# Both mixers' matmuls on pairs of float16 parts instead of pairs of float32r parts, and the first output projection's weights split during the heads

## The chip, the cores and the metric

The kernel runs on one NeuronCore of a Trainium2 chip. Its engines work side by side: TensorE (PE in the profile, with PEld for its weight loads), VectorE (DVE), ScalarE (ACT), GpSimd (POOL) and SyncE (SP, which issues most DMAs). The metric is the device time of one execution in microseconds. Lower is better.

## What is computed

Two layers of a diffusion backbone on 1024 latent tokens and 128 context tokens of width 1024. Layer 0 mixes tokens with a bidirectional gated linear recurrence, layer 1 with a chunked spatial gating; a mixture of experts (MoE) follows each. Cut to what matters here:

```python
LRU_WIDTH = 1280   # 10 heads of 128
def _rglru_mixer(h, h0, w_in, conv_w, conv_b, w_a, b_a, w_x, b_x, lam, w_out):
    proj = h @ w_in
    gate = gelu(proj[..., :LRU_WIDTH])
    xb = _centred_depthwise_conv(proj[..., LRU_WIDTH:], conv_w, conv_b)
    for d in range(2):
        r = sigmoid(einsum('bthi,hij->bthj', xh, w_a[d]) + b_a[d])
        i = sigmoid(einsum('bthi,hij->bthj', xh, w_x[d]) + b_x[d])
        log_a = -8.0 * r * softplus(-lam[d])
        u = sqrt(-expm1(2.0 * log_a)) * (i * xb)
        h_d, fin = _linear_scan(exp(log_a), u, h0[:, d], reverse=(d == 1))
    y = ((hs[0] + hs[1]) * gate) @ w_out

def _sgu_mixer(h, w_in, norm_g, w_s, b_s, w_out):
    proj = gelu(h @ w_in)                       # 1024 -> 4096
    u, v = proj[..., :2048], _rmsnorm(proj[..., 2048:], norm_g)
    sv = einsum('gpq,bnqgc->bnpgc', w_s, v) + b_s   # within chunks of 128 tokens
    return (u * sv) @ w_out                     # 2048 -> 1024
# each layer: x = x + g1 * mixer(norm(x));  x = x + g2 * moe(norm(x))
```

## The kernel before

Every product in float32 precision is made of three matmuls on two parts of each operand: hi*hi, hi*lo and lo*hi. A helper, split (and its copies in split_w, split_g and split_wo), makes the parts: ScalarE casts the raw tile to the part hi, VectorE or GpSimd subtracts hi from the raw tile to give lo. In the MoE the parts are float16 (whi, wlo, Sh, Sl, Hh, Hl; L1591 and L1597 split the weights, L1706 multiplies). In both mixers the parts are of the type F32R, four bytes each.

Mixer 0 puts channels on partitions and all 1152 tokens on columns, in three groups of 386 (with a few padding columns). After a prologue that turns and normalises x and makes the modulation, 24 modulated tiles hn are split (L116, L117), and the projections begin: product, L844 to L846, three matmuls for each of 8 blocks of the contraction and each of the 3 column groups, so 72 for one head's one half of w_in. A loop over the heads follows. In the turn of head h it projects head h+1's recurrent half (kind 1), convolves it (conv: ScalarE copies the PSUM result to xp at L869, VectorE makes xc at L871 to L873), makes head h's gate products (ri, L882 to L884, 4 x 9 matmuls) and sigmoids (L941, L943), projects head h-1's gelu half (kind 0), then ScalarE's tanh, exp and square root (L950 to L961), VectorE's decay and drive (L966 to L974), two scans (L893), their sum (L982), and the product with the gelu of head h-1 (L986, L991, L992), which GpSimd stores to DRAM as hg_d. Parts of the later modulation (mod_step) are put between. Which engine does what is fixed by the order of the code: each engine works its own instructions off in that order. The weights of w_in come in blocks of 512 KB in the order of the list "order"; load_w issues a load into one of two buffers wraw, split_w splits the oldest block and issues the next load; split_w is called twice in a head, split_g once, for the gate weights.

Behind the last head's gates stand its two projections (kind 0 of heads 8 and 9), 144 matmuls. During these and the rest of head 9, w_out's ten row blocks are loaded (wor, four buffers, L1051) and split (split_wo: ScalarE L1055, and VectorE or GpSimd L1056), each at a hand-chosen place. The output projection (ymm, L1126 to L1128) takes the tokens in 9 chunks of 128: 10 heads x 2 column halves x 3 matmuls of 512 columns. Its left operand is hg, loaded from DRAM, split, and for head 9 kept on the chip as hg9. A router and the MoE follow.

Mixer 1 puts tokens on partitions in its products uv (L1297 to L1299): 9 chunks of 128 tokens, 8 column blocks of 512, 8 contraction blocks, three matmuls each; weights sgwh and sgwl are split as they come (sgr). The v half is normalised and multiplied with the spatial weights (sv, L1406 to L1408, 256 columns), then gating with u (L1411), and the result is turned and stored to mt_d. The output projection (L1466 to L1468) makes the first 512 output columns of all chunks, then the second: for each chunk it loads m in four pieces from mt_d, splits them (L116, L117) and runs 48 matmuls of 512 columns.

## Time and profile before

| | |
|---|---|
| runs shown | 2682.14, 2679.63, 2677.31 us; median 2679.63 |
| profiled execution | 2680.47 us, of which the span from the first to the last instruction is 2678.7 |
| busy in the span | PE 2511.0 us (94%), DVE 1925.0 (72%), ACT 1631.0 (61%), POOL 310.3 (12%) |
| matmuls | 26054 |
| DMA traffic | 647 MB, 242 GB/s |
| mean granted clock of TensorE | 0.967 of the full one |

The stages by the order of time, from the profiled execution: prologue 0 to 57 us, head loop with its lead-in 57 to 421, first output projection to 571, router to 627, MoE of layer 0 to 1260, mixer 1 from 1275 to 1966, router, MoE of layer 1 from 2020 to the end.

The profile is read so: a busy share says how much of the time an engine worked, not whether the others waited for it. Matmuls are pipelined, so the listed duration of one is longer than the distance to the next; the distance between starts is the price. An idle time carries behind the arrow what ended it. Where a chain row names an engine, the end of the execution hung on it there.

### The profile page before, as it was taken

The numbers are of one execution on the slowest core, as the hardware profiler recorded it, in microseconds if no ns is written. First come the engines' busy times: TensorE is split into PE (matmuls) and PEld (weight loads), VectorE is DVE, ScalarE is ACT, GpSimd is POOL, SyncE is SP. The second block draws the span as 40 slices with busy tenths as digits, with TensorE's granted clock in tenths as the row PEclk, the third lists the DMA queues.
The fourth block names the chain that finished last, engine by engine and source line by source line (L and its number), as shares of the span: only waits on it lengthen the run. The fifth ranks groups of instructions, "written<-read, shape, count | busy, mean of one in ns | idle before, by whom it ended". The sixth has DMA issues, their size and how long they took to land.

```text
span 2678.7 us, 60563 instructions
## 1 busy us (share of the span) xinstructions
PE 2511.0 (94%) x26054; PEld 2280.8 (85%) x26054; DVE 1925.0 (72%) x2766; ACT 1631.0 (61%) x2338; POOL 310.3 (12%) x330
## 2 busy tenths in 40 slices
PE   6999998968999999997999999999969999999996
PEld 5888987858999999997777788878858999999996
DVE  6887786368999999996622233344578999989997
ACT  4766784337787877775523333333347777777774
POOL 1011003020000000001200100000120000000003
PEclk8999999978999999998999999999978999999998
DMA  8455215446999999995544433355557999999994
GB/s 305 150 183 168 69 42 198 143 186 234 360 346 359 352 350 335 352 362 165 170 157 154 160 127 110 113 186 184 175 201 283 353 359 346 356 350 338 354 350 181
DMA packets 317755, 647.19 MB, mean 242 GB/s; under 512 B 15362, under 2 KB 52790, under 8 KB 317486
## 3 DMA queue, kind: packets, MB, share of 16 engines
q1 hardware_dynamic: 291792, 564.30, 59.1%
q0 software_dynamic: 21136, 74.67, 8.7%
q10 hardware_dynamic: 4558, 4.35, 0.5%
q8 instruction: 204, 3.34, 0.5%
q14 instruction: 65, 0.53, 0.1%
HBM read 576.59 MB, written 66.68 MB: 240 GB/s over the span
## 4 chain that ended last, share of the span: by engine, by line
PE 60%; DVE 26%; ACT 7%; issue 4%; DMA 2%; POOL 1%; SPq 0%; DVEq 0%; POOLq 0%; ACTq 0%
PE mm L1706 19%; DVE wlo L1597 14%; PE uv L1297 5%; PE uv L1299 5%; PE uv L1298 5%; PE y L1466 2%; PE y L1468 2%; PE y L1467 2%; PE pj L844 2%; DVE Hl L1730 2%; PE pj L845 2%; PE pj L846 2%; DVE t L1722 2%; ACT Hh L1727 2%; PE y L1126 1%
## 5 line engine op out<-in xcount | busy, mean ns | idle before, releaser
L1706 PEld LDWEIGHTS <-whi 128*128 128x128 f16 x12288 | 990.0, 98 | 28.8 <-issue 23.9
L1597 DVE SCALAR_TENSOR_TENSOR wlo<-raw,whi 128x1024 f16<-128x1024 f32 x759 | 894.6, 1220 | 20.6 <-ACT whi L1591 20.5
L1706 PE MATMUL mm<-Sh,whi 128*128 128x144 f16 x4096 | 774.9, 227 | 3.7 <-ACT tmp L1652 1.7
L1706 PE MATMUL mm<-Sl,whi 128*128 128x144 f16 x4096 | 774.7, 226 | 1.0 <-DVE Sl L1664 0.9
L1706 PE MATMUL mm<-Sh,wlo 128*128 128x144 f16 x4096 | 774.8, 227 | 0.0
L1591 ACT ACTIVATE whi<-raw 128x1024 f16<-128x1024 f32 x759 | 755.2, 1060 | 0.0
L1706 PEld LDWEIGHTS <-wlo 128*128 128x128 f16 x6144 | 602.9, 98 | 14.3 <-issue 14.2
L1706 PE MATMUL mm<-Hh,whi 128*128 128x144 f16 x2048 | 389.9, 227 | 17.4 <-DVE Hh L1729 14.9
L1706 PE MATMUL mm<-Hl,whi 128*128 128x144 f16 x2048 | 388.7, 227 | 8.6 <-DVE Hl L1730 8.6
L1706 PE MATMUL mm<-Hh,wlo 128*128 128x144 f16 x2048 | 388.7, 227 | 0.0
L1297 PE MATMUL uv<-sgwh,h_hi 128*128 128x512 f32 x576 | 232.2, 403 | 0.0
L1299 PE MATMUL uv<-sgwh,h_lo 128*128 128x512 f32 x576 | 226.7, 393 | 0.0
L1298 PE MATMUL uv<-sgwl,h_hi 128*128 128x512 f32 x576 | 225.8, 392 | 0.0
L1303 ACT ACTIVATE uvo<-uv 128x512 f32<-128x512 f32 x72 | 43.0, 597 | 217.2 <-PE uv L1299 217.2
L1750 POOL DMA_INDIRECT x_d<-o,idx x31 | 57.9, 1869 | 959.7 <-ACT o L1749 928.6
L844 PE MATMUL pj<-hn_hi,wh 128*128 128x386 f32 x480 | 164.6, 343 | 1.9 <-ACT hn_hi L116 1.9
L846 PE MATMUL pj<-hn_hi,wl 128*128 128x386 f32 x480 | 164.1, 342 | 0.0
L845 PE MATMUL pj<-hn_lo,wh 128*128 128x386 f32 x480 | 163.9, 341 | 0.0
L1411 DVE SCALAR_TENSOR_TENSOR uvo<-sv,bs,uvo 128x256 f32<-128x256 f32 x72 | 31.5, 479 | 156.1 <-PE sv L1408 156.1
L1297 PEld LDWEIGHTS uv<-sgwh,h_hi 128*128 128x128 f32 x576 | 109.2, 189 | 31.4 <-ACT uvo L1303 10.1
L1299 PEld LDWEIGHTS uv<-sgwh,h_lo 128*128 128x128 f32 x576 | 108.8, 189 | 24.4 <-DVE h_lo L1290 0.4
L1316 DVE TENSOR_TENSOR uvo<-uvo,gain 128x512 f32<-128x512 f32 x36 | 24.9, 691 | 145.4 <-ACT uv L1315 145.4
(398 smaller groups left out, 4253.8 us busy)
## 6 DMA issues: line engine op xcount, KB each, us to landing
raw<-in_moe_w_gate_dram SPq DMA_DIRECT2D x64, 2048.0 KB
raw<-in_moe_w_up_dram SPq DMA_DIRECT2D x64, 2048.0 KB
raw<-in_moe_w_down_dram SPq DMA_DIRECT2D x62, 2048.0 KB
wm<-in_w_mod_dram SPq DMA_DIRECT2D x96, 512.0 KB
m<-mt_d SPq DMA_DIRECT2D x72, 256.0 KB
sgr<-in_sg_w_in_dram SPq DMA_DIRECT2D x32, 512.0 KB
win<-in_lru_w_in_dram SPq DMA_DIRECT2D x20, 512.0 KB
v_d<-uvo POOLq DMA_DIRECT2D x36, 256.0 KB, 2.5
```

What stands on the lines that cost most here:

```text
L844: PE.matmul(ps[:, i, 0:WP], wh[:, k], hi[k][:, cs], start=(k == 0), stop=False)
L845: PE.matmul(ps[:, i, 0:WP], wh[:, k], lo[k][:, cs], start=False, stop=False)
L846: PE.matmul(ps[:, i, 0:WP], wl[:, k], hi[k][:, cs], start=False, stop=(k == KD - 1))
L1297: PE.matmul(ps, hi[:, k, cs], th[:, k % 4], start=(k == 0), stop=False)
L1298: PE.matmul(ps, hi[:, k, cs], tl[:, k % 4], start=False, stop=False)
L1299: PE.matmul(ps, lo[:, k, cs], th[:, k % 4], start=False, stop=(k == KD - 1))
L1466: PE.matmul(ps, mh, th[:, j], start=(q == 0 and j == 0), stop=False)
L1467: PE.matmul(ps, mh, tl[:, j], start=False, stop=False)
L1591: A.activation(hi, block(n, b), AF.Copy, scale=UP)
L1597: V.scalar_tensor_tensor(lo, block(n, b), UP, ws[n, b][0], op0=OP.mult, op1=OP.subtract)
L1706: PE.matmul(ps[:, b, 0:144], w[:, k], x[:, k], start=(k == 0 and i == 0), stop=(k == KD - 1 and i == 2))
L1750: G.indirect_dma_start(out=x_d[0:NS, :], out_offset=bass.IndirectOffsetOnAxis(ap=idxs[:, e:e + 1], axis=0), in_=o, in_offset=None, compute ...
```

## The change

All matmul operands in the two mixers become pairs of float16 tiles. A new helper, split_up, scales while it splits: hi = float16(raw * by) on ScalarE, lo = raw * by - hi on VectorE as one instruction with two operations. Weights are scaled by UP (2 to the 8th), hg and m by DOWN (2 to the -4th); 1/UP comes back in the activations that read PSUM (conv, gates, both gelus), 1/(UP*DOWN) in the multiplications with the gate row of the residual and in the prompt chunk's copies (take). Where GpSimd does the subtraction, ScalarE scales the raw tile in place first and then casts it. In mixer 1, bs is scaled instead of copied, mt copied with a scale, the square for the norm gets a float32 tile of its own (junk1), and the weights of a block lie in one tile.

The output projection's weights become blocks of kind 2 of the list of loads: three wraw buffers, and in each head one more call of split_w behind the sum of the scans; one more after the loop. load_wo and split_wo are gone, with their places at the end. The pool of w_out's parts (l0o) is opened in front of the heads' pool. The first two weight blocks and the first gate block are split in one place, ahead of the modulated tiles.

```diff
+    def split_up(raw, hi, lo, by=UP, eng=V):
+        if eng is G:
+            A.activation(raw, raw, AF.Copy, scale=by)
+            A.copy(hi, raw)
+            G.tensor_tensor(lo, raw, hi, op=OP.subtract)
+            return
+        A.activation(hi, raw, AF.Copy, scale=by)
+        V.scalar_tensor_tensor(lo, raw, by, hi, op0=OP.mult, op1=OP.subtract)
...
-            V.tensor_mul(yps, yps, self.g1)
+            V.scalar_tensor_tensor(yps, yps, 1.0 / (UP * DOWN), self.g1, op0=OP.mult, op1=OP.mult)
...
-                    A.copy(t[:, cs[n]], yps[n])
+                    A.activation(t[:, cs[n]], yps[n], AF.Copy, scale=1.0 / (UP * DOWN))
...
-        order = [(1, 0), (1, 1)] + [b for h in range(1, NH - 1) for b in ((1, h + 1), (0, h - 1))]
-        order += [(0, NH - 2), (0, NH - 1)]
+        WRAW = 3
+        order = [(1, 0), (1, 1), (1, 2), (0, 0), (2, 0)]
+        order += [b for h in range(1, NH - 2) for b in ((1, h + 2), (0, h), (2, h))]
+        order += [(0, NH - 2), (0, NH - 1), (2, NH - 2), (2, NH - 1)]
+        whl = {}
...
+                if kind == 2:
+                    SP.dma_start(raw[b].rearrange("p k n -> p (k n)"), lru_w_out[0, rows(h)])
+                else:
+                    SP.dma_start(raw[b], win[:, :, kind * LW + P * h:kind * LW + P * (h + 1)])
-        def split_w(copy=A.copy, eng=V):
+        def split_w(eng=V):
             if to_split:
                 kind, h = b = to_split.pop(0)
-                wh = wp.tile([P, KD, P], F32R, tag="whi", name=f"wh{kind}_{h}", bufs=2)
-                wl = wp.tile([P, KD, P], F32R, tag="wlo", name=f"wl{kind}_{h}", bufs=2)
-                copy(wh, raw[b])
-                eng.tensor_tensor(wl, raw.pop(b), wh, op=OP.subtract)
-                ready[b] = wh, wl
+                if kind == 2:
+                    whl[h] = [op_.tile([P, D], F16, name=f"wo{s}{h}") for s in "hl"]
+                    split_up(raw.pop(b).rearrange("p k n -> p (k n)"), *whl[h])
+                else:
+                    wh = wp.tile([P, KD, P], F16, tag="whi", name=f"wh{kind}_{h}", bufs=2)
+                    wl = wp.tile([P, KD, P], F16, tag="wlo", name=f"wl{kind}_{h}", bufs=2)
+                    split_up(raw.pop(b), wh, wl, eng=eng)
+                    ready[b] = wh, wl
...
-        split_w(eng=G)
+        for _ in range(2):
+            split_w(G)
+        gg = split_g(0, G)
...
-        hi, lo = zip(*([hp.tile([P, W], F32R, name=f"hn_{s}{k}") for s in ("hi", "lo")] for k in range(KD)))
+        hi, lo = zip(*([hp.tile([P, W], F16, name=f"hn_{s}{k}") for s in ("hi", "lo")] for k in range(KD)))
...
-            if u == 3:
-                split_w(G.tensor_copy, G)
-        gg = split_g(0, G)
...
-            A.activation(flat(xp[:, 2:W + 2]), ps[:, :, 0:WP], AF.Identity)
+            A.activation(flat(xp[:, 2:W + 2]), ps[:, :, 0:WP], AF.Identity, scale=1.0 / UP)
...
             c.scan(1)
             c.add()
+            split_w()
             if h > 0:
                 G.dma_start(hg_d[h - 1], gated(h - 1, gt))
...
+        split_w()
         norm_cols(0, 2)
...
-        for i in range(4):
-            load_wo(i)
...
-        split_wo(0, G)
         gt = gelu(NH - 2, gps[0])
...
         c.scan(1)
-        split_wo(1, G)
         c.add()
-        split_wo(2, V)
-        split_wo(3, V)
-        split_wo(4, G)
         gt = gelu(NH - 1, gps[1])
-        split_wo(5, V)
         t = gated(NH - 1, gt)
...
-        split_wo(6, G)
-        split_wo(7, V)
-        split(t, *hg9)
+        split_up(t, *hg9, DOWN)
...
-        split_wo(8, G)
-        split_wo(9, V)
...
-        hi = hp.tile([P, KD, NT], F32R, name="h1_hi")
-        lo = hp.tile([P, KD, NT], F32R, name="h1_lo")
+        hi = hp.tile([P, KD, NT], F16, name="h1_hi")
+        lo = hp.tile([P, KD, NT], F16, name="h1_lo")
...
-            t = raw.pop((i, r))
-            A.copy(th, t)
-            eng.tensor_tensor(tl, t, th, op=OP.subtract)
+            split_up(raw.pop((i, r)), th, tl, eng=eng)
...
-            A.activation(o, ps, AF.Gelu_apprx_tanh)
+            A.activation(o, ps, AF.Gelu_apprx_tanh, scale=1.0 / UP)
...
-            A.copy(mt, ps.rearrange("p a b -> p (a b)"))
+            A.activation(mt, ps.rearrange("p a b -> p (a b)"), AF.Copy, scale=DOWN / UP)
```

VectorE at the end of one of the late turns of the head loop, before: wl is the low part of a block of w_in, hv the two scans, hs first their sum (L982) and then, of the head before, the product with the gelu; xc begins the next convolution.

```order
L647 TENSOR_TENSOR wl_7_3040<-win_7_2777,wh_7_3039 128x1024
L893 SCALAR_TENSOR_TENSOR hv_1_3045<-tau_1_2998,par,ti_1_2910 128x1024
L893 SCALAR_TENSOR_TENSOR hv_1_3045<-tau_1_2998,ti_1_2910 128x128
L982 TENSOR_TENSOR hs_3049<-hv_0_3033,hv_1_3045 128x1152
L991 TENSOR_TENSOR hs_2783<-hs_2783,gt_3031 128x1024
L992 TENSOR_TENSOR hs_2783<-hs_2783,gt_3031 128x128
L871 TENSOR_SCALAR xc_3131<-xp_3127,par 128x1158
```

The same place now, with the lines of the changed kernel (wol is the low part of a block of w_out):

```order
L127 SCALAR_TENSOR_TENSOR wl_7_3090<-win_7_2821,wh_7_3089 128x1024
L913 SCALAR_TENSOR_TENSOR hv_1_3095<-tau_1_3048,par,ti_1_2960 128x1024
L913 SCALAR_TENSOR_TENSOR hv_1_3095<-tau_1_3048,ti_1_2960 128x128
L1002 TENSOR_TENSOR hs_3099<-hv_0_3083,hv_1_3095 128x1152
L127 SCALAR_TENSOR_TENSOR wol_3102<-win_7_2833,woh_3101 128x1024
L1011 TENSOR_TENSOR hs_2827<-hs_2827,gt_3081 128x1024
L1012 TENSOR_TENSOR hs_2827<-hs_2827,gt_3081 128x128
L891 TENSOR_SCALAR xc_3187<-xp_3183,par 128x1158
```

One subtraction now stands between the sum and the gelu product; on ScalarE the cast woh stands behind the last cast wh, ahead of the next xp.

ScalarE at the end of the heads, before: tau is head 9's last step there, woh are casts of blocks of w_out, gt the gelus of heads 8 and 9, hgh the high parts of what the output projection multiplies, hg9h those of head 9.

```order
L970 ACTIVATE tau_1_3561<-tau_1_3561 128x1158
L1055 CAST woh_3557<-wor_3531 128x1024
L986 ACT_TABLE_LOAD
L986 ACTIVATE gt_3581<-pj_8_3368 128x1158
L116 CAST hgh_3589<-hgl_3529 128x1024
L116 CAST hgh_3589<-hs_3306 128x128
L1055 CAST woh_3555<-wor_3533 128x1024
L1055 CAST woh_3539<-wor_3535 128x1024
L1055 CAST woh_3541<-wor_3537 128x1024
L1055 CAST woh_3543<-wor_3579 128x1024
L986 ACTIVATE gt_3620<-pj_9_3441 128x1158
L1055 CAST woh_3545<-wor_3604 128x1024
```

The same place now:

```order
L990 ACTIVATE tau_1_3596<-tau_1_3596 128x1158
L1006 ACT_TABLE_LOAD
L1006 ACTIVATE gt_3612<-pj_8_3434 128x1158
L126 ACTIVATE hgh_3620<-hgl_3592 128x1024
L126 ACTIVATE hgh_3620<-hs_3364 128x128
L1006 ACTIVATE gt_3635<-pj_9_3507 128x1158
L126 ACTIVATE hg_xh<-hs_3633 128x1152
```

The casts of w_out are gone from the end; the gelu of head 9 follows directly on the last small part of hgh.

## Rows read from the trace of the kernel before

**Rows 1.** Page: the chain that ended last, share of the span by engine.

```profile
PE 60%; DVE 26%; ACT 7%; issue 4%; DMA 2%; POOL 1%; SPq 0%; DVEq 0%; POOLq 0%; ACTq 0%
```

**Rows 2.** Windows: us of the span, busy us (instructions) per engine, PEclk, DMA share, GB/s.

```profile
421.00:446.00 25.00, 17.05 (x59) 12.26 (x58) 19.79 (x13) 11.90 (x12) 15.07 (x7) 0.86 0.72 240
...
627.00:1262.00 635.00, 618.29 (x9601) 610.62 (x9599) 571.03 (x768) 490.73 (x670) 50.04 (x32) 0.99 0.93 331
```

**Rows 3.** Lines by shape: line, engine, operation, tiles, count, busy us, mean ns, idle before.

```profile
L1706 PEld LDWEIGHTS <-whi 128*128 128x128 f16 x12288 | 990.0, 98 | 28.8 <-issue 23.9 <-DVE Sh L1661 3.2 <-DVE pt L1737 1.2
...
L1297 PE MATMUL uv<-sgwh,h_hi 128*128 128x512 f32 x576 | 232.2, 403 | 0.0
...
L844 PE MATMUL pj<-hn_hi,wh 128*128 128x386 f32 x480 | 164.6, 343 | 1.9 <-ACT hn_hi L116 1.9
...
L1466 PE MATMUL y<-sgwh,m_3hl 128*128 128x512 f32 x72 | 29.3, 407 | 0.1
```

**Rows 4.** TensorE in order of time: start us, duration us, line, tiles; pairs for pitches.

```profile
395.48 0.34 PE L846 MATMUL pj<-hn_hi,wl 128*128 128x386 f32 x1
...
420.38 0.33 PE L846 MATMUL pj<-hn_hi,wl 128*128 128x386 f32 x1
...
446.40 0.39 PE L1127 MATMUL y<-wol,hgh 128*128 128x512 f32 x1
...
452.81 0.40 PE L1128 MATMUL y<-woh,hg9l 128*128 128x512 f32 x1
...
1249.83 0.23 PE L1706 MATMUL mm<-Hh,whi 128*128 128x144 f16 x1
...
1252.45 0.38 PE L1744 MATMUL oTT<-ident,oT 128*128 128x128 f32 x2
...
1514.11 0.39 PE L1299 MATMUL uv<-sgwh,h_lo 128*128 128x512 f32 x1
...
1521.59 0.40 PE L1299 MATMUL uv<-sgwh,h_lo 128*128 128x512 f32 x1
```

**Rows 5.** Waits from 86 to 396 us (total, times, longest), then ScalarE in order.

```profile
ACT xp L869 <- PE pj L846: 67.5, 8, 9.9
...
DVE tau L966 <- ACT sq L961: 39.3, 9, 4.9
...
328.73 1.14 ACT L869 ACTIVATE xp<-pj 128x1158 f32<-128x1158 f32 x1 [6.69 <-PE pj L846]
...
361.55 1.14 ACT L869 ACTIVATE xp<-pj 128x1158 f32<-128x1158 f32 x1 [6.68 <-PE pj L846]
```

**Rows 6.** Lines by shape: splits of weight blocks in the MoE and in mixer 0.

```profile
L1597 DVE SCALAR_TENSOR_TENSOR wlo<-raw,whi 128x1024 f16<-128x1024 f32 x759 | 894.6, 1220 | 20.6 <-ACT whi L1591 20.5
...
L1591 ACT ACTIVATE whi<-raw 128x1024 f16<-128x1024 f32 x759 | 755.2, 1060 | 0.0
...
L647 DVE TENSOR_TENSOR wl<-win,wh 128x1024 fp32r<-128x1024 f32 x18 | 22.0, 1221 | 10.5 <-ACT wh L646 10.5
```

**Rows 7.** Order of time at the end of the heads: ScalarE, TensorE, then VectorE.

```profile
420.73 3.88 ACT L1055 CAST woh<-wor 128x1024 fp32r<-128x1024 f32 x4
...
425.69 0.80 PE L1126 MATMUL y<-woh,hgh 128*128 128x512 f32 x1 [4.28 <-ACT gt L986]
...
410.92 4.32 DVE L893 TENSOR_TENSOR_SCAN hv<-tau,par,ti 128x1024 f32<-128x1024 f32 x1
...
421.06 2.35 DVE L893 TENSOR_TENSOR_SCAN hv<-tau,par,ti 128x1024 f32<-128x1024 f32 x1
```

**Rows 8.** VectorE in order of time, mixer 1's output projection, first half of columns.

```profile
1769.19 0.69 DVE L262 TENSOR_TENSOR y<-y,g 128x512 f32<-128x512 f32 x1
...
1816.30 0.69 DVE L262 TENSOR_TENSOR y<-y,g 128x512 f32<-128x512 f32 x1
```

**Rows 9.** VectorE and ScalarE in order of time, ahead of the first projection.

```profile
47.98 2.32 DVE L776 TENSOR_SCALAR sp<-par 128x20 f32<-128x20 f32 x1
...
56.22 0.71 ACT L808 ACTIVATE hn<-hT,modc,ns 128x386 f32<-128x386 f32 x1 [8.38 <-DVE ns L188]
```

More of the change, by code (lines that the diff above doesn't have):

```diff
@@ L275, in residual @@
             cs = slice(512 * n, 512 * (n + 1))
-            V.tensor_mul(t[:, cs], yps, self.g1 if self.apart else self.g1[:, cs])
+            V.scalar_tensor_tensor(t[:, cs], yps, 1.0 / (UP * DOWN), self.g1 if self.apart else self.g1[:, cs],
+                                   op0=OP.mult, op1=OP.mult)
             V.tensor_add(xt[:, cs], xt[:, cs], t[:, cs])
@@ L686, in lru_mixer @@
             mod0.load(k)
-        for _ in range(2):
+        for _ in range(WRAW):
             load_w()
@@ L829, in lru_mixer @@
         e1.close()
+        op_ = pool_of(es, "l0o")
         tp = pool_of(es, "l0t")
@@ L874, in conv @@
                                        op0=OP.mult, op1=OP.add)
-            return xc, tmp("xh", f"xh{h}", dt=F32R), tmp("xl", f"xl{h}", dt=F32R)
+            return xc, *(tp.tile([P, W], F16, tag=tag, name=f"{tag}{h}", bufs=1) for tag in ("xh", "xl"))
         def ri(h, d, j, xh, xl, gh, gl):
@@ L940, in gates @@
                     tr = self.tr[d] = tmp("tr", f"tr{h}_{d}", 2)
-                    A.activation(flat(tr), ri(h, d, 0, xh, xl, *gg)[:, :, 0:WP], AF.Sigmoid, bias=par_of(50, d, h))
+                    A.activation(flat(tr), ri(h, d, 0, xh, xl, *gg)[:, :, 0:WP], AF.Sigmoid, bias=par_of(50, d, h), scale=1.0 / UP)
                     ti = self.ti[d] = tmp("ti", f"ti{h}_{d}", 2)
-                    A.activation(flat(ti), ri(h, d, 1, xh, xl, *gg)[:, :, 0:WP], AF.Sigmoid, bias=par_of(70, d, h))
+                    A.activation(flat(ti), ri(h, d, 1, xh, xl, *gg)[:, :, 0:WP], AF.Sigmoid, bias=par_of(70, d, h), scale=1.0 / UP)
                     V.tensor_mul(ti, ti, xc)
@@ L985, in gelu @@
             gt = tmp("gt", f"gt{h}")
-            A.activation(flat(gt), gps[:, :, 0:WP], AF.Gelu_apprx_tanh)
+            A.activation(flat(gt), gps[:, :, 0:WP], AF.Gelu_apprx_tanh, scale=1.0 / UP)
             return gt
@@ L1042, in lru_mixer @@
         carry = carry_of(0)
-        eo, ew = ExitStack(), ExitStack()
+        ew = ExitStack()
         pb = pool_of(ew, "l0b", side="right")
-        op_ = pool_of(eo, "l0o", 1, side="right")
-        whl, wor, hgs = {}, {}, {}
-        def load_wo(h):
-            if h < NH:
-                wor[h] = op_.tile([P, D], F32, tag="wor", name=f"wor{h}", bufs=4)
-                SP.dma_start(wor[h], lru_w_out[0, rows(h)])
-        def split_wo(h, eng):
-            wh, wl = whl[h]
-            A.copy(wh, wor[h])
-            eng.tensor_tensor(wl, wor[h], wh, op=OP.subtract)
-            load_wo(h + 4)
+        hgs = {}
         def load_hg(ch, h0=0, h1=9):
@@ L1065, in split_hg @@
         def split_hg(ch):
-            hh = tmp("ae", f"hgh{ch}", 2, F32R)[:, 0:9 * P].rearrange("p (h t) -> p h t", t=P)
-            hl = tmp("hs", f"hgo{ch}", 2, F32R)[:, 0:9 * P].rearrange("p (h t) -> p h t", t=P)
-            split(hgs[ch], hh, hl)
+            hh = tmp("ae", f"hgh{ch}", 2, F16)[:, 0:9 * P].rearrange("p (h t) -> p h t", t=P)
+            hl = tmp("hs", f"hgo{ch}", 2, F16)[:, 0:9 * P].rearrange("p (h t) -> p h t", t=P)
+            split_up(hgs[ch], hh, hl, DOWN)
             return hh, hl
@@ L1072, in lru_mixer @@
         SP.dma_start(hgs[0][:, 0:8], hg_d[0:8, :, rows(0)].rearrange("h p t -> p h t"))
-        for i in range(4):
-            load_wo(i)
-        for h in (*range(2, NH), 1, 0):
-            whl[h] = [op_.tile([P, D], F32R, name=f"wo{s}{h}") for s in "hl"]
         c.tanh()
@@ L1259, in norm @@
             for i, ch in enumerate(chs):
-                A.activation(hi[:, :, rows(ch)], xs[ch].rearrange("p (k t) -> p k t", k=KD), AF.Square,
-                             accum_out=ss[:, i:i + 1])
+                A.activation(junk, xs[ch], AF.Square, accum_out=ss[:, i:i + 1])
             r = sm.tile([P, 2], F32, tag="rstd2", name=f"rstd1_{chs[0]}")
```

46 lines of the change are left out of this document (22 added, 24 removed).

## The prediction, made before the changed kernel was run

> **What bounds the kernel now.** I read three views first. The chain that ended last gives TensorE 60% of the span and VectorE 26% [rows 1]; most of the VectorE part is the splitting of the experts' weights in the two MoE stages, which the change doesn't touch: there the windows show TensorE and VectorE busy side by side and the DMA engines at 0.93 [rows 2]. In the two mixers the chain runs through the matmul lines. The lines kept apart by shape then say how many matmuls of which width there are, all on four-byte operands [rows 3], and the order of time says how far apart two of them start [rows 4]. A listed mean (343 ns for 386 columns) is a latency, since matmuls overlap; what counts is the pitch from start to start.
>
> Pitches at the full clock [rows 4]: 386 columns, (420.38 - 395.48)/141 steps = 176.6 ns; 512 columns in the gating mixer, (1521.59 - 1514.11)/33 = 226.7 ns; in the first output projection, (452.81 - 446.40)/28 = 228.9 ns; 144 float16 columns in the MoE, (1252.45 - 1249.83)/42 = 62.4 ns. At TensorE's upper level, 2.4 GHz, one column per cycle would take 160.8, 213.3, 213.3 and 60.0 ns. So the four-byte matmuls lose 13 to 16 ns each, the float16 one 2.4 ns.
>
> The head loop of mixer 0 is bound by TensorE as well: ScalarE waits for the projection in front of a head's first step (L869), 67.5 us in 8 waits of up to 9.9 us, 6.69 us before one of the shortest heads, and VectorE waits 39.3 us in 9 waits in front of L966 [rows 5]. The shortest heads follow each other at 361.55 - 328.73 = 32.8 us [rows 5].
>
> **Matmuls on float16.** The change keeps the number of matmuls and columns and changes the operand width. No row of before shows a float16 matmul of 386 or 512 columns. The nearest is the 144-column one. Either what it loses over its columns is fixed (2.4 ns), so that 386, 256 and 512 columns take 163.2, 109.1 and 215.7 ns; or it grows with the width (62.4/60.0), which gives 167, 111 and 222 ns; at best nothing is lost, 160.8, 106.7 and 213.3. I take the fixed one: it is the middle of the three, and the three four-byte pitches lose about the same (13.4, 15.6, 15.8 ns) whatever their width. Saved per matmul: 13.4 ns at 386 columns, 11.0 in the gating mixer, 13.2 in the first output projection. For the 256-column ones (216) I show no pitch; they lie between 0 and 11 ns, I take 7.
>
> The Trainium skill, "TensorE: Matmul & The Clock Gate", section Back-to-back issue gap, gives N/2.4 + 2.5 ns from one matmul to the next, a fixed loss; by it the estimate would be the sum below, about 66 us, where a loss that grows would leave about 43. The 62.4 ns of the 144 columns [rows 4] agrees with it (62.5), but one width can't tell the two apart.
>
> Now by stage, for the profiled execution of 2680.5 us (span 2678.7 and 1.8 us around it; 0.8 above the median of 2679.6):
>
> Head loop. The projections are 3 x 480 matmuls of 386 columns (L844 to L846, of which one line is shown) [rows 3], 144 per head. Seven full head periods save 144 x 13.4 = 1.9 us, and about 0.3 more of the 36 gate matmuls (4 x 9 in the code), the rest of whose 0.5 ScalarE's gates hide: 7 x 2.2 = 15.4. The first 144, before the loop, reach the chain with 1.3; head 0, half as many, with 1.2. Together 17.9 us. Against this stands the added split of one weight block per head: a cast on ScalarE, 1.06 us, and a subtraction on VectorE, 1.22 us by the nearest forms, those of the MoE's splits [rows 6], and one load on SP's queue. ScalarE has 6.7 us of waiting in front of its next step there. VectorE meets the split behind the sum of a head's two scans, ahead of the gating product and the next convolution; they come 1.2 us later, and the wait in front of L966 (39.3/9 = 4.4 us) takes that up. In the shortest heads VectorE then needs 32.8 - 4.4 + 1.2 = 29.6, TensorE 32.8 - 2.2 = 30.6. So I cost the splits at nothing, but the cover left is about 1 us. Splits that were there cost the same: VectorE's old form takes 1221 ns, the new 1220 [rows 6].
>
> End of the heads. Before, ten blocks of the output projection's weights are loaded and split while the projection waits for them: ScalarE casts four in a row (3.88 us) ahead of the last head's gelu, TensorE stands 4.28 us for that gelu and goes on at the lower clock at first (0.86 in this stretch), and waits again behind splits on GpSimd; a scan that takes 2.35 us in one direction takes 4.32 in the other, beside such a split [rows 2, 7]. The sixty matmuls of token chunk 0 begin behind the last projection (420.38) and end just ahead of 446.40, at 446.1 [rows 4]. After, none of this stands there. What is late next is ScalarE's order: its small cast waits for the gated product of head 8 (VectorE, two scans behind), then comes the last gelu, near 420.1 in before's times, since VectorE gains some 2 us from the undisturbed scan. From there the 57 matmuls that are left x 215.7 ns end at 432.4. Gain 446.1 - 432.4, say 13.6 us, 1.9 of it the 144 projections. If the old wait remains in another form, half is lost: 7.
>
> Rest of the output projection. Chunks 1 to 8 have 60 matmuls each (10 heads x 2 halves x 3), 480, with TensorE without a wait: 480 x 13.2 ns = 6.3 us (3.4 if the loss grows with the width).
>
> Mixer 1. uv (L1297 to L1299): 3 x 576 x 11.0 ns = 19.0 us [rows 3], TensorE without waits in this stretch. Spatial product: 216 (3 for each of 72 results in the code) x 7 = 1.5. Output projection: 12 lines like the one shown, of 72 = 864 matmuls [rows 3]. The second half of its columns is bound by TensorE: 8 x 48 x 11.0 = 4.2. In the first half, chunks follow one another at (1816.30 - 1769.19)/4 = 11.8 us [rows 8] where 48 matmuls need 10.9, so a loop of stores and loads sets part of that pace; between 0 and 4.7, I take 2.1. Together 26.8 us.
>
> Start. The first splits go to one place ahead of the modulated input, with GpSimd's subtractions earlier; before, a VectorE step on 20 columns takes 2.32 us beside them, twice [rows 9]. ScalarE gets three scalings and some casts more, about 5.3 us (1.06 us for each of the four at 1024 columns [rows 6], half for the two at 512), in a wait of 8.38 us [rows 9]. Between 4 us gained and 1.4 lost; I take 2 gained.
>
> The scalings ride on instructions that exist (activation scale, a multiplication that becomes a multiply-multiply on the same operands): nothing. The router and MoE stages move as a block.
>
> Sum: 17.9 + 13.6 + 6.3 + 26.8 + 2.0 = 66.6 us; 2680.5 - 66.6 = 2613.9. Against the median: 2613 to 2614.
>
> **Rivals.**
> A. The float16 loss grows with the width. Then a head saves 1.6 instead of 2.2, uv 8, the projections 3.4 and 3, the rest as above: about 43 us, 2637. For it: no row of such width. Against: the four-byte losses don't grow.
> B. The heads go over to the chain of VectorE and ScalarE: the wait in front of L966 follows ScalarE's sq, so it is not VectorE's spare time if ScalarE is late too. Then the seven periods keep nothing or lose a little: 15 us less, 2629. The two cases together give about 2648.
> C. The end of the heads keeps a wait (the gelu stays behind something, the clock falls again): 7 us less, 2621; within the range.
> D. Slower: the float16 weight load can't be hidden. It takes 98 ns [rows 3]; each of the 5148 changed matmuls (1440 + 360 + 540 in mixer 0, 1728 + 216 + 864 in mixer 1) has its own. The saving per matmul in the sum is about 10 ns; with the 20 us from elsewhere the change turns slower once more than some 13 ns of each load stand open. In full it would add about 98 ns to each pitch of 163 or 216: some 430 us more than before, 3110. Against it: in the MoE the same loads stand behind matmuls of 62.4 ns, shorter than the load, and pitch is 62.4 all the same [rows 3, 4].
> The Trainium skill, "TensorE: Matmul & The Clock Gate", section The mechanism, says in its list of what overlaps that a weight load runs beside matmuls only when it goes to another row group; all of these use the full array, so by that sentence D would happen, though the section also knows of a background buffer for weights. The trace disagrees with the sentence: 98 ns loads, 62.4 ns pitch.
> E. More than forecast: no loss at all and the loop of mixer 1's first half following TensorE, and the start at its best: 10 us for the loss (5148 x 2.4 ns, less what is hidden), 2.6 and 2 for the others, 2600.
> F. No gain that can be measured, the savings all being given back as waits at stage ends: 2680.
>
> **How the numbers follow.** Forecast with C 0.62, A 0.12, B 0.11, both 0.04, E 0.06, D 0.03, F 0.02. The likeliest gives 2614. From 2600 to 2640 the range holds the forecast, C, B, A and most of E, over 0.8; the ends are E and A with a little of the start's bounds. A measurement here can tell about 0.2% (5 us) from no change. Faster: everything but D and F, 0.95, less 0.01 for A and B with the start lost, 0.94; slower 0.03; same 0.03.
>
> **What would show it.** Pitches in the trace of after: 163 and 216 ns is right, 167 and 222 is A, over 230 is D. Head periods of 34.2 (full heads) and 30.6 (the shortest) with ScalarE still waiting for the projection before L869's counterpart: right; a wait of TensorE in front of the gate matmuls or the projection in its place: B. TensorE's stand of about 1.5 us at the end of the heads, without falling to the lower clock, and chunk 0 over about 13 us after its first matmul: right. uv's stretch 19 us shorter. The MoE stages must be as long as before; if they are longer, what I called moved as a block is wrong. The forecast fails at once if the matmuls turn out to have waits inside accumulation groups.

## The result and the profile after

The changed kernel takes 2601.97 us (median of four, 2598.56 to 2603.85), the kernel before beside it 2680.55. The ratio is 0.9707, 95% interval 0.969 to 0.9724: 2.9% faster. The prediction was 2614, range 2600 to 2640. The profiled execution has a span of 2599.0 us against 2678.7; that difference of 79.7 us is what is split up here, where the sum of the prediction was 66.6.

The share of each engine from the page, and then lines kept apart by shape, which answer to [rows 3]:

```profile
PE 2431.4 (94%) x26054; PEld 1850.1 (71%) x26054; DVE 1914.7 (74%) x2771; ACT 1640.6 (63%) x2348; POOL 293.2 (11%) x324
...
L1290 PE MATMUL uv<-sgw,h_hi 128*128 128x512 f16 x576 | 219.4, 381 | 0.0
...
L864 PE MATMUL pj<-hn_hi,wh 128*128 128x386 f16 x480 | 158.2, 330 | 1.9 <-ACT hn_hi L116 1.9
...
L1290 PEld LDWEIGHTS <-h_hi 128*128 128x128 f16 x576 | 56.5, 98 | 69.4 <-issue 10.0 <-ACT uvo L1296 1.7 <-ACT sgr L122 0.8
```

There are as many matmuls as before, those of the two mixers on float16; a weight load takes 98 ns where the four-byte ones took 189. The latencies (381 for 403, 330 for 343) say little; the pitch does. TensorE in order of time, as in [rows 4]:

```profile
374.02 0.33 PE L866 MATMUL pj<-hn_hi,wl 128*128 128x386 f16 x1
...
397.07 0.33 PE L866 MATMUL pj<-hn_hi,wl 128*128 128x386 f16 x1
...
411.08 0.38 PE L1121 MATMUL y<-woh,hgh 128*128 128x512 f16 x1
...
416.91 0.38 PE L1121 MATMUL y<-woh,hg_xh 128*128 128x512 f16 x1
```

386 columns: (397.07 - 374.02)/141 = 163.5 ns; 512 columns: (416.91 - 411.08)/27 = 215.9 ns. At a granted clock of 1.00 in both stretches, 386 and 512 columns at 2.4 GHz are 160.8 and 213.3 ns; the loss over that is 2.6 ns at both widths. So it is fixed, and rival A falls with the trace alone.

The span, cut at the same instructions in both profiled executions (in us, from the first matmul of each stage to that of the next):

| stage | before | after | change | forecast |
|---|---|---|---|---|
| start, to the first projection | 57.4 | 56.9 | -0.5 | -2.0 |
| projections and heads, to the first output projection | 363.2 | 340.4 | -22.8 | -19.8 |
| token chunk 0 of the output projection | 25.5 | 13.8 | -11.7 | -11.7 |
| chunks 1 to 8 and router, to the first MoE matmul | 179.3 | 169.9 | -9.4 | -6.3 |
| MoE 0 and the first turn of x in mixer 1 | 644.9 | 642.8 | -2.1 | 0 |
| mixer 1: uv and spatial product | 479.8 | 453.9 | -25.9 | -20.5 |
| mixer 1: output projection | 219.2 | 211.5 | -7.7 | -6.3 |
| the rest, with MoE 1 | 709.4 | 709.8 | +0.4 | 0 |

Nothing in this table has the wrong sign. The start gained less than forecast; everywhere else where it misses, the gain was put too small, above all where many matmuls stand between other work of TensorE. A second profiled execution of the changed kernel gives the same stages within 0.6 us, with one exception: its first projection starts at 54.8 us. Over the kernels below that leave the start alone, the first projection starts anywhere from 54.8 to 58.1 us, so the row of the start is the reading of one execution, and its -0.5 can't be told from 0 or from the forecast.

The head loop, ScalarE in order of time (compare [rows 5]); first the starts of two full heads before the change, then four starts after it:

```profile
259.66 1.14 ACT L869 ACTIVATE xp<-pj 128x1158 f32<-128x1158 f32 x1 [9.88 <-PE pj L846]
...
295.91 1.14 ACT L869 ACTIVATE xp<-pj 128x1158 f32<-128x1158 f32 x1 [9.89 <-PE pj L846]
```

```profile
245.51 1.14 ACT L889 ACTIVATE xp<-pj 128x1158 f32<-128x1158 f32 x1 [6.87 <-PE pj L866]
...
279.14 1.14 ACT L889 ACTIVATE xp<-pj 128x1158 f32<-128x1158 f32 x1 [6.87 <-PE pj L866]
...
309.74 1.14 ACT L889 ACTIVATE xp<-pj 128x1158 f32<-128x1158 f32 x1 [3.86 <-PE pj L866]
...
340.33 1.14 ACT L889 ACTIVATE xp<-pj 128x1158 f32<-128x1158 f32 x1 [3.86 <-PE pj L866]
```

The shortest heads follow at 30.6 us, as forecast, and a full one takes 33.6 or 34.1 us in turn (34.2 forecast), where it took 36.3 or 36.7; ScalarE still waits for the projection. VectorE's wait ahead of the decay step is the cover of the added split. In the shortest heads it was 3.96 us before:

```profile
347.27 2.64 DVE L966 SCALAR_TENSOR_TENSOR tau<-ae,tau 128x1158 f32<-128x1158 f32 x2 [3.96 <-ACT sq L961]
```

After the change it is 0.59 us there (second row) and 3.01 in a full head (first row):

```profile
297.34 2.64 DVE L986 SCALAR_TENSOR_TENSOR tau<-ae,tau 128x1158 f32<-128x1158 f32 x2 [3.01 <-ACT sq L981]
...
327.94 2.64 DVE L986 SCALAR_TENSOR_TENSOR tau<-ae,tau 128x1158 f32<-128x1158 f32 x2 [0.59 <-ACT sq L981]
```

The end of the heads, which answers to [rows 7]: ScalarE's small cast, the last gelu, and TensorE's wait for it.

```profile
396.97 0.31 ACT L126 ACTIVATE hgh<-hs 128x128 f16<-128x128 f32 x1 [5.81 <-DVE hs L1011]
397.49 1.14 ACT L1006 ACTIVATE gt<-pj 128x1158 f32<-128x1158 f32 x1 [0.21 <-PE pj L866]
...
398.67 0.38 PE L1121 MATMUL y<-woh,hgh 128*128 128x512 f16 x1 [0.63 <-ACT gt L1006]
```

The gelu stands behind the small cast as the prediction said, and TensorE now waits 0.63 us for it instead of 4.28. It keeps the full clock: the granted clock is 1.00 from 397 to 411 us, where it was 0.50 from 426 to 430 before, and the matmul in the last row takes the 0.38 us of its neighbours, where the one of before took 0.80.

### The profile page after: what moved, and what is told of

Its sections match the earlier page's. It is cut to its first block, busy times and chain, and to the rows that moved or that the text cites. A ratio compares the mean times of both kernels' runs of the same rounds, so it can differ in the third digit from the quotient of the medians.

```text
span 2599.0 us, 60553 instructions
## 1 busy us (share of the span) xinstructions
PE 2431.4 (94%) x26054; PEld 1850.1 (71%) x26054; DVE 1914.7 (74%) x2771; ACT 1640.6 (63%) x2348; POOL 293.2 (11%) x324
## 5 line engine op out<-in xcount | busy, mean ns | idle before, releaser
L1698 PEld LDWEIGHTS <-whi 128*128 128x128 f16 x12288 | 989.1, 98 | 30.6 <-issue 24.2
L1290 PE MATMUL uv<-sgw,h_hi 128*128 128x512 f16 x576 | 219.4, 381 | 0.0
L1291 PE MATMUL uv<-sgw,h_hi 128*128 128x512 f16 x576 | 219.3, 381 | 0.0
L1292 PE MATMUL uv<-sgw,h_lo 128*128 128x512 f16 x576 | 219.1, 380 | 0.0
L864 PE MATMUL pj<-hn_hi,wh 128*128 128x386 f16 x480 | 158.2, 330 | 1.9 <-ACT hn_hi L116 1.9
L865 PE MATMUL pj<-hn_lo,wh 128*128 128x386 f16 x480 | 157.8, 329 | 0.1
L866 PE MATMUL pj<-hn_hi,wl 128*128 128x386 f16 x480 | 157.9, 329 | 0.0
L1644 ACT ACTIVATE tmp<-xgT,modc,ns 128x128 f32<-128x128 f32 x248 | 90.2, 468 | 47.5 <-PE xgT L1631 38.8
L1709 ACT ACTIVATE sg<-mm 128x288 f32<-128x288 f32 x128 | 52.3, 409 | 94.5 <-PE mm L1698 94.3
```

The source lines that it names most:

```text
L864: PE.matmul(ps[:, i, 0:WP], wh[:, k], hi[k][:, cs], start=(k == 0), stop=False)
L865: PE.matmul(ps[:, i, 0:WP], wh[:, k], lo[k][:, cs], start=False, stop=False)
L866: PE.matmul(ps[:, i, 0:WP], wl[:, k], hi[k][:, cs], start=False, stop=(k == KD - 1))
L1290: PE.matmul(ps, hi[:, k, cs], th[:, k % 4], start=(k == 0), stop=False)
L1291: PE.matmul(ps, hi[:, k, cs], tl[:, k % 4], start=False, stop=False)
L1292: PE.matmul(ps, lo[:, k, cs], th[:, k % 4], start=False, stop=(k == KD - 1))
```

## The experiments

All kernels are edits of the changed one. Its median in the first comparison is 2602.0, in a later one 2603.5, and its nine executions lie between 2598.6 and 2604.2 us. A difference of under some 3 us can't be read from whole times alone; where one matters, the stages of the traces are given beside it.

**The type alone, in mixer 1.**

The same edit is made for wsh, wsl, the weight tiles and the pairs of v and m. Two smaller things of the change go back with it: junk1 is gone and the square for the norm is written into hi again, and a tile that the steps behind the output projection use (hT) lies among the weight tiles again.

```diff
-        hi = hp.tile([P, KD, NT], F16, name="h1_hi")
-        lo = hp.tile([P, KD, NT], F16, name="h1_lo")
+        hi = hp.tile([P, KD, NT], F32R, name="h1_hi")
+        lo = hp.tile([P, KD, NT], F32R, name="h1_lo")
```

> The changed kernel with mixer 1's matmul operands back at the four-byte type F32R, with the same scalings, tile shapes and order as in the changed kernel. Theory (mixer 1's gain is the pitch of the matmuls alone, more than forecast because four-byte matmuls lose 0.1 us more after each interruption by transposes): uv's stretch is back at about 480 us instead of 454 and the output projection at 219 instead of 211.5, whole 2633 to 2637; in the trace the second matmul after transposes starts 0.3 us after the first, the others 0.227. Rival (part of the gain is from the order, the one tile for the weights or the norm's own tile): the whole stays 5 us or more under that, 2620 to 2630.

Measured: 2634.92 us (2633.32 to 2636.1), ratio to before 0.9832 (0.9816 to 0.9849). This is inside the theory's 2633 to 2637; the rival's 2620 to 2630 is out. In the trace uv and the spatial product take 478.1 us again (479.8 before the change, 453.9 after) and the output projection 219 (219.2 and 211.5). So mixer 1's gain is the type of its operands, and not the order, the scalings or the one tile for the weights, which stay in this kernel. The norm's own tile goes back together with the type and isn't parted from it. What the four-byte type costs at an interruption stands in the order of time; ahead of each stretch four transposes (x4), first in this kernel, then in the changed one:

```profile
1506.91 0.60 PE L1410 MATMUL mT<-ident,uvo 128*128 128x128 f32 x4
1507.27 0.48 PE L1290 MATMUL uv<-sgw,h_hi 128*128 128x512 f32 x1
1507.58 0.40 PE L1291 MATMUL uv<-sgw,h_hi 128*128 128x512 f32 x1
1507.82 0.40 PE L1292 MATMUL uv<-sgw,h_lo 128*128 128x512 f32 x1
```

```profile
1484.46 0.60 PE L1410 MATMUL mT<-ident,uvo 128*128 128x128 f32 x4
1484.90 0.38 PE L1290 MATMUL uv<-sgw,h_hi 128*128 128x512 f16 x1
1485.11 0.38 PE L1291 MATMUL uv<-sgw,h_hi 128*128 128x512 f16 x1
1485.33 0.38 PE L1292 MATMUL uv<-sgw,h_lo 128*128 128x512 f16 x1
```

With four-byte operands the second matmul behind the transposes starts 0.31 us after the first, and the third 0.24 us after the second; with float16 it is 0.21 and 0.22. Here much of that comes back, since the first one starts 0.36 us after the transposes instead of 0.44. Over all of uv a loss remains: the 1635 distances between two of its matmuls with no other one between them average 233.8 ns before, 233.1 in this kernel and 217.4 in the changed one, 16.4 ns of difference instead of the 11.0 of the forecast, while the 92 distances with other matmuls between them sum to 90.9, 90.0 and 91.6 us. The pitch of [rows 4] was read in a stretch without interruption, and left this out.

**The splits of w_out at the end again.**

load_wo and split_wo are back at their places of before, on float16 parts and with all subtractions on VectorE; w_out's blocks are out of the list of loads again.

```diff
             c.add()
-            split_w()
...
+        for i in range(4):
+            load_wo(i)
...
+        split_wo(0, V)
         gt = gelu(NH - 2, gps[0])
...
         c.scan(1)
+        split_wo(1, V)
         c.add()
+        split_wo(2, V)
+        split_wo(3, V)
+        split_wo(4, V)
         gt = gelu(NH - 1, gps[1])
+        split_wo(5, V)
         t = gated(NH - 1, gt)
+        split_wo(6, V)
+        split_wo(7, V)
...
+        split_wo(8, V)
+        split_wo(9, V)
```

The first kernel of this kind, with the pool of the raw buffers opened where the heads' weights and operands had lain:

> The changed kernel with one part undone: w_out's ten blocks are again loaded and split at the end of the heads, at the places of before, on float16 parts; all ten subtractions are on VectorE (before: five on GpSimd). Theory (the 11.8 us that token chunk 0 lost came from these loads and splits): the gelu of head 9 stands behind four casts again, 4 us, blocks 6 to 9 come late by DMA; chunk 0 takes 22 to 25 us from its first matmul instead of 13.7, and the whole is 8 to 12 us slower than the changed kernel, 2610 to 2614. Rival (it came from the smaller operands and from the contention with GpSimd, which is not there in this kernel): chunk 0 at most 17 us, whole at most 2606.

Measured: 2621.69 us (2620.0 to 2623.3), 18 to 20 more than the changed kernel and outside both expectations. The trace says why: the raw buffers lay where the projections' operands had been, so the loads were issued at 397.66 us, when the last projection had ended, and not some 16 us ahead of it as before; TensorE stood 8.3, 5.7 and 3.2 us. So it measured something else. The second kernel of this kind has `orp = pool_of(es, "l0r")` opened beside l0o, ahead of the heads, and two raw buffers for the heads' weights instead of three:

> As the first run with w_out's splits at the end, but the four raw buffers have a place of their own, so that the loads are issued some 16 us ahead of the output projection, as before the change, and not only when the last projection has read its operands (two raw buffers for the heads' weights, as before the change). All ten subtractions on VectorE. Theory (chunk 0 lost its 11.8 us to these loads and splits): head 9's gelu behind four casts, 4 us of standing, blocks 6 to 9 late; chunk 0 takes 20 to 25 us from its first matmul instead of 13.7; whole 6 to 11 us more than the changed kernel, 2608 to 2613. Rival (smaller operands and no GpSimd there): chunk 0 at most 17 us, whole at most 2606.

Measured: 2610.44 us (2610.11 to 2610.85), ratio to before 0.9739 (0.9722 to 0.9755): 7 to 8.4 us more than the changed kernel. ScalarE and TensorE at this place, order of time:

```profile
397.84 3.88 ACT L126 ACTIVATE woh<-wor 128x1024 f16<-128x1024 f32 x4
401.63 1.11 ACT L1006 ACTIVATE gt<-pj 128x1158 f32<-128x1158 f32 x1
405.54 1.06 ACT L126 ACTIVATE woh<-wor 128x1024 f16<-128x1024 f32 x1 [2.80 <-DMA wor<-in_lru_w_out_dram]
...
402.79 0.59 PE L1148 MATMUL y<-woh,hgh 128*128 128x512 f16 x1 [5.83 <-ACT gt L1006]
...
418.31 0.27 PE L1167 MATMUL finT<-ident,fin 128*20 128x128 f32 x1
```

Again the gelu stands behind four casts, TensorE stands for it (5.8 us) and comes back slower (0.59 us for a matmul, a granted clock of 0.57 from 403 to 407 us), and the later blocks wait for their loads. Chunk 0 takes from 396.2 to 418.3, 22.2 us instead of 13.7 to the same row, on float16 and with no subtraction on GpSimd. So the place of the splits is worth some 8 of the 11.7 us. Of the other 3, the smaller operands are 0.8 (60 x 13 ns). TensorE's waits in chunk 0 behind the subtractions (total, times, longest) make up about the rest; first before the change, on GpSimd, then in this kernel, on VectorE:

```profile
PE y L1127 <- POOL wol L1056: 3.7, 3, 1.9
```

```profile
PE y L1149 <- DVE wol L127: 1.1, 2, 0.9
```

They are 2.6 us shorter here. No kernel changes GpSimd's share alone.

**The cover of the added split.** Extra copies of the split of each w_out block, into tiles that nobody reads:

```diff
+                    for x in range(1):
+                        split_up(raw[b].rearrange("p k n -> p (k n)"), *(tp.tile([P, D], F16, tag=f"dup{s}", name=f"dup{s}{x}_{h}", bufs=1) for s in "hl"))
                     split_up(raw.pop(b).rearrange("p k n -> p (k n)"), *whl[h])
```

The second kernel has range(2).

> The changed kernel with the added split of each head made twice, the second time into a tile that nobody reads: 1.05 us on ScalarE and 1.22 us on VectorE more in each head. Theory (the heads are bound by TensorE, the splits lie in VectorE's wait ahead of the decay step, 3.0 us or more in the full heads and 0.6 in the two shortest): full heads unchanged at 33.6 to 34.1 us, the two shortest 0.6 longer each; whole 0 to 2.5 us more than the changed kernel. Rival (VectorE and ScalarE already set the heads' pace): 1.2 us for each head, 11 to 12 us more.

> The same with two extra splits in each head (2.1 us on ScalarE, 2.44 on VectorE). Theory: full heads still unchanged or up to 0.3 longer (2.44 against a wait of 3.0 to 3.6), the two shortest 1.9 longer each, the end up to 1 us; whole 3 to 6 us more than the changed kernel. Rival (VectorE sets the pace): 22 to 24 us more.

Measured: 2617.28 and 2678.94 us, 14 to 15 and 75 to 77 us more than the changed kernel: both are far above the theory and above the rival too. Both have a wait of their own, though: with one scratch buffer ScalarE's next copy waits for VectorE to read the last one. ScalarE in the kernel with one extra split, ahead of head 9's gates, where two blocks are split in a row:

```profile
379.13 1.06 ACT L126 ACTIVATE duph<-win 128x1024 f16<-128x1024 f32 x1 [8.98 <-DVE dupl L127]
...
382.55 1.21 ACT L963 ACTIVATE tr<-ri,par 128x1158 f32<-128x1158 f32 x1
```

The heads themselves kept their pace in it; the 9 us are ScalarE held in its order behind a buffer, and TensorE stands 10.6 us ahead of the gates for the sigmoid that follows. With two extra splits ScalarE waits so 11 times, 93 us in all, and projections and heads take 417 us instead of 340. So these two say what one missing buffer between ScalarE and VectorE costs, and nothing on the cover. With three scratch buffers, and none for the last two blocks:

> One extra split in each head as before, but into three scratch buffers instead of one, and none for the last two blocks, so that ScalarE never waits for a scratch tile. Theory (heads bound by TensorE): full heads 33.6 to 34.1 us as in the changed kernel, the two shortest 0 to 0.6 longer; whole 0 to 2 us more. Rival (VectorE and ScalarE set the pace): 1.2 us for each of eight heads, 10 us more.

> Two extra splits in each head, into three scratch buffers, none for the last two blocks: 2.1 us on ScalarE and 2.44 on VectorE more. Theory: full heads 0 to 0.3 longer (VectorE's wait there is 3.0 to 3.6), the two shortest 1.2 to 1.9 longer; whole 2 to 6 us more than the changed kernel. Rival: 2.4 us for each of eight heads, 20 us more.

Measured: 2604.65 (2603.46 to 2605.48) and 2607.03 us (2604.76 to 2608.18), 1 to 3 and 3.5 to 5 us more than the changed kernel. ScalarE's steps with two extra splits:

```profile
247.33 1.14 ACT L891 ACTIVATE xp<-pj 128x1158 f32<-128x1158 f32 x1 [4.98 <-PE pj L868]
...
280.96 1.14 ACT L891 ACTIVATE xp<-pj 128x1158 f32<-128x1158 f32 x1 [4.98 <-PE pj L868]
...
311.55 1.14 ACT L891 ACTIVATE xp<-pj 128x1158 f32<-128x1158 f32 x1 [1.97 <-PE pj L868]
...
342.58 1.14 ACT L891 ACTIVATE xp<-pj 128x1158 f32<-128x1158 f32 x1 [1.18 <-PE pj L868]
```

Full heads are at 33.6 and 34.1 us as without them, the shortest at 30.6 and 31.0 (1.2 to 1.9 us longer were expected); only one early head is longer, by about 1 us, and the end. The rival's 20 us did not come: the heads are bound by TensorE, and even three splits a head hide. In the shortest heads VectorE's wait of 0.59 us is gone in this kernel, and TensorE keeps its pace all the same, so some of VectorE's work must run on into the next head. Only two heads are so short; whether a longer row of them would hold the pace isn't shown.

**An earlier start.** In the changed kernel VectorE works off the softplus ahead of the modulation's bias, beside GpSimd's two subtractions (48.86 to 53.09 us); VectorE, then TensorE:

```profile
49.06 1.98 DVE L797 TENSOR_TENSOR sp<-sp,sp 128x20 f32<-128x20 f32 x1
51.08 2.04 DVE L798 TENSOR_SCALAR sp<-sp 128x20 f32<-128x20 f32 x1
...
53.85 1.11 PE L184 MATMUL modT<-ident,modb 128*128 128x128 f32 x4 [5.43 <-DVE modb L174]
56.86 0.48 PE L864 MATMUL pj<-hn_hi,wh 128*128 128x386 f16 x1 [1.90 <-ACT hn_hi L116]
```

Before, two other steps beside GpSimd took 2.3 us each [rows 9]; now these two take 2.0, so the long steps only moved, and the start gained 0.5 us and not 2. In the second profiled execution of the changed kernel GpSimd began 0.9 us later; the softplus was over by then, at 0.17 to 0.18 us a step, and the steps behind the modulation's bias were the long ones. GpSimd, then VectorE:

```profile
49.75 4.21 POOL L124 TENSOR_TENSOR wl<-win,wh 128x1024 f16<-128x1024 f32 x2 [14.68 <-ACT wh L123]
...
52.01 3.40 DVE L832 TENSOR_SCALAR hn<-hT,ns,modc 128x386 f32<-128x386 f32 x2
```

The two steps of L832 took 0.87 us together in the first execution. The first projection starts at 54.8 us there instead of 56.9: which of VectorE's steps meet GpSimd's subtractions differs between executions, and the gain of the start with it.

```diff
-        V.tensor_mul(q[2], q[2], q[0])
-        V.tensor_scalar(q[3], lam, -1.0, 0.0, op0=OP.mult, op1=OP.max)
-        V.tensor_add(q[2], q[2], q[3])
-        V.tensor_scalar_mul(sp4, q[2], 4.0)
-        V.tensor_scalar_mul(sp8n, q[2], -8.0)
...
         mod0.end()
+        split_w()
         mod0.cols()
...
-        for _ in range(2):
-            split_w(G)
-        gg = split_g(0, G)
...
+            if u == 3:
+                split_w()
+        gg = split_g(0)
```

The five steps stand again behind the modulated tiles, and q's tiles lie in a pool that is open until there.

> The changed kernel with another order ahead of the first projection: the modulation's bias, turn and scale come before the last five steps of the softplus on VectorE (these go behind the modulated tiles), and the first splits are on VectorE, one ahead of the modulated tiles and the others among and behind them, none on GpSimd. Theory (the first projection waits for VectorE's small steps, two of which stand beside GpSimd's subtractions for 2 us each): the first projection starts at 52.5 to 54 us instead of 56.9, the whole 2 to 5 us less than the changed kernel, 2597 to 2600, part of it given back by the 1.8 us more on VectorE among the modulated tiles. Rival (the start is set by the loads of the modulation's weights, TensorE's part ends at 48.4 us): under 1.5 us less.

Measured: 2598.80 us (2598.22 to 2599.36), 3 to 5 us less than the two medians of the changed kernel, whose fastest execution of 2598.6 is as fast. TensorE there:

```profile
48.43 0.66 PE L184 MATMUL modT<-ident,modb 128*128 128x128 f32 x4 [1.08 <-DVE modb L174]
51.28 0.32 PE L865 MATMUL pj<-hn_hi,wh 128*128 128x386 f16 x1 [2.20 <-ACT hn_hi L116]
```

The first projection starts at 51.3 us, earlier than the theory's 52.5 to 54. This is 5.6 us earlier than in the execution shown first and 3.6 earlier than in the second, the earliest of those that keep the order. Head 9's convolution is 2.2 and 3.6 us earlier than in the two executions of the changed kernel; 1.4 and 2.0 us go back among the modulated tiles. So the earlier start is shown; what it is worth in the whole is 2 to 5 us, near the least that whole times can tell. The edit moves VectorE's steps and takes the subtractions from GpSimd; these two aren't parted.

**The loop in mixer 1's output projection.**

```diff
-                xt = self.xt[ch] = self.pool.tile([P, 512], F32, tag="xh", name=f"pxh{self.l}_{ch}", bufs=2)
+                xt = self.xt[ch] = self.pool.tile([P, 512], F32, tag="xh", name=f"pxh{self.l}_{ch}", bufs=4)
...
-            return kp.tile([P, 512], F32, tag="q", name=name, bufs=3)
+            return kp.tile([P, 512], F32, tag="q", name=name, bufs=6)
...
-            return kp.tile([P, 2, 512], F16, tag="pm", name=name, bufs=4)
+            return kp.tile([P, 2, 512], F16, tag="pm", name=name, bufs=6)
...
+                split_m(2)
+                load_m(4)
+                load_m(5)
+                load_m(6)
...
-            split_m(c + 2)
-            load_m(c + 4)
+            split_m(c + 3)
+            load_m(c + 7)
```

> The changed kernel with more buffers in mixer 1's output projection: four instead of two for the halves of x that SyncE fetches, six instead of three and four for the pieces of m, which are loaded three and split one further ahead. Theory (in the first half of the columns a loop of stores, fetches and loads on SyncE's queue sets the pace of the first chunks, 11.9 us each where 48 matmuls need 10.4, and took the gain of the shorter matmuls there): those chunks follow at 10.4 to 10.8 us, 4 to 6 us less than the changed kernel. Rival (the pace is set by the transfer of m itself, or by ScalarE and VectorE in it): under 1.5 us less.

Measured: 2590.31 us (2587.57 to 2593.99), 12 to 13 less by the medians, 9.1 less by the spans of the profiled executions. That is about twice the 4 to 6 us of the theory, and the trace has it in the stage that was meant: the output projection is 9.4 us shorter. VectorE at the end of a chunk, first in the changed kernel, then with the buffers (compare [rows 8]):

```profile
1708.24 0.69 DVE L272 SCALAR_TENSOR_TENSOR y<-y,g 128x512 f32<-128x512 f32 x1
...
1744.46 0.69 DVE L272 SCALAR_TENSOR_TENSOR y<-y,g 128x512 f32<-128x512 f32 x1
...
1781.37 0.70 DVE L272 SCALAR_TENSOR_TENSOR y<-y,g 128x512 f32<-128x512 f32 x1 [1.20 <-PE y L1460]
```

```profile
1720.35 0.70 DVE L272 SCALAR_TENSOR_TENSOR y<-y,g 128x512 f32<-128x512 f32 x1 [3.51 <-PE y L1464]
1730.71 0.70 DVE L272 SCALAR_TENSOR_TENSOR y<-y,g 128x512 f32<-128x512 f32 x1 [3.66 <-PE y L1464]
...
1772.15 0.70 DVE L272 SCALAR_TENSOR_TENSOR y<-y,g 128x512 f32<-128x512 f32 x1 [3.65 <-PE y L1464]
```

12.1 us a chunk before the buffers ((1744.46 - 1708.24)/3), 10.36 with them, which is 48 x 215.9 ns: TensorE sets the pace, and VectorE waits for it. The theory had counted a few chunks at 11.9 us. In the changed kernel the second chunk took 13.9 us from its first matmul to the next one's, and the four after it 11 to 13; all of them take 10.4 here. So in the first half of the columns the change itself had left nearly all of its gain lying. In the queue of SyncE, from 1675 to 1785 us, the waits that stood there in the changed kernel:

```profile
SPq L267 <- DMA x_d<-pxh: 21.5, 6, 3.6
SPq L1426 <- DMA m<-mt_d: 21.4, 8, 4.3
```

The first, a fetch that waits until the half of x two chunks back has been stored, holds up the loads of m queued behind it; with the buffers both waits are gone. Whether the four buffers for x do it alone, or the deeper loading and splitting of m too, was not tried apart.

**Both together, beside the changed kernel.**

> The changed kernel itself once more, beside the two versions built on it: 2600 to 2604.

> The earlier start and the buffers of mixer 1's output projection together. If the two are independent: the sum, 3 us and 4 to 6 us, 2593 to 2596.

Measured: the changed kernel 2603.52 us (2599.63 to 2604.19), both together 2588.39 us (2587.2 to 2590.52), ratio to before 0.9661 (0.9647 to 0.9675). This beats both kernels: 91 us less than before, 15 less than the changed one. It is less than the 2593 to 2596 expected, because the buffers gave more; the earlier start adds some 2 us to them (2588.4 against 2590.3), and there the ranges of the executions overlap.

## Why the prediction was right, step by step

- **The pitch of float16 matmuls** (fixed loss, 163.2 and 215.7 ns): right, 163.5 and 215.9. The formula of the Trainium skill ("TensorE: Matmul & The Clock Gate", section Back-to-back issue gap) gives 163.3 and 215.8 and holds here at both widths. The prediction leaves out that the section calls this the gap of isolated matmuls and gives about 131 ns at 512 columns for a sustained stream of weight loads and matmuls; in the stream here it is 215.9.
- **What the four-byte matmuls had cost**: too small, and this is the term that leaves most of the 12 us between the forecast and the result. I took the pitch from a stretch without interruption [rows 4]. Over chunks 1 and 2 of the first output projection the mean distance of two matmuls in a row was 235 ns before and 216 after, 19 ns instead of 13: 480 x 19 = 9.1 us, near the measured 9.4. In uv it is 16.4 ns instead of 11.0, and with F32R back in the same order the loss comes back, so there it is the type; whether it is the longer weight load (189 against 98 ns) or the wider moving operand was not tried.
- **The heads**: the shortest heads right to 0.1 us; a full head gained 2.6 instead of 2.2. In the traces its projections gained 2.1 us (1.9 forecast) and its 36 gate products 0.6, which I had put at 0.3, the rest behind ScalarE. That rest does stand behind ScalarE in the shortest heads: TensorE waits 1.0 us there for a sigmoid ahead of the gates (0.8 before), the small beginning of what rival B describes. The split in each head at no cost: right, and shown with one and two more. Rival B falls, since ScalarE still waits for the projection in every full and short head.
- **The end of the heads**: right, 11.7 us, and the wait that remains is 0.6 us where about 1.5 was forecast; undoing the place alone gives 8 of them back.
- **Mixer 1's output projection**: the total was near, its parts were not. The first half of the columns gained 1.2 us (103.7 from 104.9, from its first matmul to the last product), not 2.1, because the loop on SyncE's queue set the pace; the second half gained 6.5 instead of 4.2 by the pitch. The two misses partly cancel, so that the total came near is luck.
- **The start**: -0.5 instead of -2 in the execution shown. VectorE's long steps beside GpSimd were moved, not removed, and where they fall differs between executions by more than the forecast.
- **MoE 0 and the turn of mixer 1**: -2.1 where I had nothing. TensorE waits 8.6 us instead of 11.2 for the first normalised x: GpSimd's subtraction came later, behind ScalarE's added scaling, and a VectorE step on 2 columns that had taken 2.32 us beside it takes 0.16.
- **The total**: 2602 lies near the lower end of the range, which the prediction had given to rival E, no loss at all, the loop of mixer 1 following TensorE and the best start. None of the three came. The time came so low mainly because the four-byte matmuls had cost more than their pitch in an uninterrupted stretch, which stands in no rival.
- **Rival D**, the weight load that can't be hidden: falls. The loads take 98 ns, and the pitches of 163 and 216 ns are the columns plus 2.6. The sentence of the Trainium skill ("TensorE: Matmul & The Clock Gate", section The mechanism) that a load overlaps only another row group is against the trace here too.

## What to carry to other kernels

Read a pitch over the whole stage and with all its interruptions, not in its cleanest stretch: here part of the price of the operand type showed only where matmuls change places with others. When a stage's matmuls get shorter, look for the queue that was just behind them: here a loop on SyncE's queue kept the gain of half a projection, and more buffers with earlier loads gave 9 us. An experiment that doubles a cost needs buffers of its own, else it measures the buffer. And read a stage from two executions before explaining half a microsecond of it.

## What the runs showed of the hardware that was not expected

After four transposes the second four-byte matmul of 512 columns starts 0.31 us after the first, the second float16 one 0.21; without interruption the four-byte ones stand 0.227 to 0.229 apart, the float16 ones 0.216. A stand of TensorE of 0.63 us at the end of the heads left the granted clock at 1.00, the full 2.4 GHz, where the stands of 4.28 us before and 5.83 us in the experiment were followed by 0.50 and 0.57 over the next 4 us, matmuls of 0.80 and 0.59 us instead of 0.39 and 0.38. VectorE steps beside a GpSimd subtraction of 1024 columns took longer: two on 20 columns 2.0 us each instead of 0.18, two on 386 columns 3.40 instead of 0.87 together.
